# Moving the a22 weights' split parts within a partition: high part to the other weights' offset, half of the low part to its old place

## The chip, the cores and the metric

The kernel runs on one core of one Trainium2 chip. The metric is device microseconds of one execution, as the median of several executions. In the kernel, matrix products are done by TensorE (PE in the profile; PEld is its weight load), elementwise work by VectorE (DVE), ScalarE (ACT) and GpSimd (POOL). SyncE (SP), ACT and POOL issue DMA transfers. SBUF is the on-chip memory with 128 partitions; where a tile lies is a byte offset that is the same in every partition.

## The reference

One decoder block over 512 positions of 1024 channels, in float32. The part that matters here is the gated feed-forward at its end; what stands before it (norm, projection, short convolution, sparse attention, merge) is left out.

```
h  = rmsnorm(x, norm2_g)
gu = h @ w_ffn_in                       # 1024 -> 2 * 2816
g  = causal_dwconv(gu[..., :D_FF], ffn_conv_w) + ffn_conv_b
x  = x + (silu(g) * gu[..., D_FF:]) @ w_ffn_out
```

## The kernel before

Each float32 operand is split into a high part, rounded to the type that TensorE takes at full rate, and a low part, which is the rest. A product of two such operands is three matmuls: high by high, high by low and low by high. The function `dense` (lines 437, 438 and 440) issues them: first, for each tile of 128 contracted channels, weights' high part by the moving high part (L437) and by the moving low part (L438), then, for all tiles again, weights' low part by the moving high part (L440).

The first product of the feed-forward is done two feed-forward tiles (of 128 channels) at a time in a scheme of Strassen's kind: the weights of a pair are four quarters a11, a12, a21 and a22, of which four sums are formed as well, and the tokens' activations lie in seven forms in `xf_h` and `xf_l`, each four tiles of 256 columns. A pair is then seven products instead of eight; each product is 4 x 3 = 12 matmuls of 256 columns, so a pair is 84 matmuls. There are 11 steps of f (0, 2, ... 20) with two pairs each: n = 0 for the gate half and n = 1 for the up half, 22 pairs.

`ff_forms(f, n)` makes a pair's weights. Raw weights come by DMA into `wr_s`. The quarter a22 gets its own tiles: high part `th`, low part `tl`, each 512 float32 wide (2,048 bytes per partition) with two buffers, made by `dma_split` (L173, L174 and L175: an ACT copy, an ACT copy with the sign turned, and a DMA that adds the raw weights to it). a11 and a12 lie in `wh_s` and `wl_s`; the four sums lie in `sh` and `sl`. `ff_pair` then issues the seven products, and a22 comes first: eight matmuls with `th` (four tiles, each by `xf_h` and by `xf_l`) and four with `tl` (by `xf_h` alone), then a11, a12 and the sums. The pair f = 0, n = 0 is done in another order, with matmuls put between those of the product before (L1039 and L1045).

From f = 4 on, a part of the down product, `pdn`, with weights in `wh_d` and `wl_d` and 512 moving columns, stands between two pairs: 24 matmuls. The order of instructions on each engine is found by the framework's scheduler when the program is made. It leaves some early pairs interleaved with each other and with the down product; from 443.9 us on the pairs follow each other in the plain order.

The pool `pw` holds `th`, `tl`, `sh`, `sl` and some smaller tiles. Its tiles are placed in the order in which their tags are first named, one behind the other. `th` is named first, at line 903, then a gap of 48 float32 (192 bytes), so that within the pool `th` lies at byte 0 and 2,048, the gap at 4,096, `tl` at 4,288 and 6,336 and `sh` from 8,384 on. The other weights are at the same offset modulo 512 as `tl` and `sh`.

```
pw = ctx.enter_context(tc.tile_pool(name="pw", bufs=1, side="left"))
pw.tile([P, D // 2], F32R, name="th_", tag="th", bufs=2)
const([P, 48], "gap_w", F32, pw)
```

Of the kernel before, what the change touches and what calls it, by code (L numbers as in the profile page):

```python
# [11 lines left out]
F32 = mybir.dt.float32  # L12
F32R = mybir.dt.float32r
# [5 lines left out]
P = 128  # L19
D = 1024  # L20
# [65 lines left out]
def tile_block(ctx: ExitStack, tc: tile.TileContext, xT, pos, par, par2, w_tok, w_a3, w_gate, w_ao, w_bo, w_o,  # L86
# [13 lines left out]
    def const(shape, name, dt=F32, pool=sb):  # L100
        return pool.tile(shape, dt, name=name, tag=name)
# [64 lines left out]
    def split(h, l, v):  # L166
        hi = nc.scalar.activation(h, v, AF.Copy)  # L167
        nc.vector.tensor_sub(l, v, h.bitcast(F32))  # L168
        return hi

    def dma_split(h, l, raw, src, dst=None):

        nc.scalar.activation(h, raw, AF.Copy)  # L173
        nc.scalar.activation(l, raw, AF.Copy, scale=-1.0)  # L174
        nc.gpsimd.dma_start(l if dst is None else dst, src, accum_op=ALU.add)  # L175

    def ring(name):
        return (wf.tile([P, D], F32R, name=f"wh_{name}", tag="wh", bufs=NWF),
                wf.tile([P, D], F32R, name=f"wl_{name}", tag="wl", bufs=NWF))

    def raw_tile(name):
        return wf.tile([P, D], F32, name=f"wr_{name}", tag="wr", bufs=NRAW)
# [717 lines left out]
    xf_h = const([P, 4, 7, TH], "xf_h", F32R, px)  # L900
    xf_l = const([P, 4, 7, TH], "xf_l", F32R, px)
    pw = ctx.enter_context(tc.tile_pool(name="pw", bufs=1, side="left"))
    pw.tile([P, D // 2], F32R, name="th_", tag="th", bufs=2)
    const([P, 48], "gap_w", F32, pw)

    def x_forms(k, v):
        nc.vector.tensor_sub(v[:, T1:T3 + 1], v[:, 1:4:2], v[:, 0:2])
# [57 lines left out]
        nc.scalar.activation(cv, cv, AF.Silu)  # L965

    HALF_D = D // 2

    def ff_forms(f, n):

        nm = f"{n}_{f}"
        raws = {}
        for m in (1, 0):
            raws[m] = raw_tile(f"s{nm}{m}")
            nc.sync.dma_start(raws[m], w_ff[f + m, n])
        a11, a12 = raws[0][:, 0:HALF_D], raws[0][:, HALF_D:]
        a21, a22 = raws[1][:, 0:HALF_D], raws[1][:, HALF_D:]
        form = {}
        h = pw.tile([P, HALF_D], F32R, name=f"th{nm}", tag="th", bufs=2)
        l = pw.tile([P, HALF_D], F32R, name=f"tl{nm}", tag="tl", bufs=2)  # L980
        dma_split(h, l, a22, w_ff[f + 1, n][:, HALF_D:])
        form["a22"] = (h, l)
        h, l = ring(f"s{nm}")
        dma_split(h, l, raws[0], w_ff[f, n])
        form["a11"] = (h[:, 0:HALF_D], l[:, 0:HALF_D])
        form["a12"] = (h[:, HALF_D:], l[:, HALF_D:])

        def put(i, j, v):
            h = pw.tile([P, D], F32R, name=f"sh{i}{j}{nm}", tag="sh", bufs=NSQ)
            l = pw.tile([P, D], F32R, name=f"sl{i}{j}{nm}", tag="sl", bufs=NSQ)  # L990
            split(h, l, v)
            form[i] = (h[:, 0:HALF_D], l[:, 0:HALF_D])
            form[j] = (h[:, HALF_D:], l[:, HALF_D:])

        s = {}

        def pair(i, j):
            v = pw.tile([P, D], F32, name=f"s{i}{j}{nm}", tag="sf", bufs=NSF)
            s[i], s[j] = v[:, 0:HALF_D], v[:, HALF_D:]
            return v  # L1000

        v = pair(2, 3)
        nc.vector.tensor_sub(s[3], a11, a21)
        nc.vector.tensor_sub(s[2], a22, s[3])
        put(2, 3, v)
        v = pair(4, 1)
        nc.vector.tensor_sub(s[4], a12, s[2])
        nc.vector.tensor_add(s[1], a21, a22)
        put(4, 1, v)
        return form  # L1010
# [51 lines left out]
    def ff_strassen(f, between):  # L1062
        u = u_bufs[f // 2 % NU]

        with tc.high_priority(offset=AHEAD if f == 0 else 0):
            form = ff_forms(f, 0)
        ff_pair(f, 0, u[:, :, 2:], form, late=f == 0 or None)
        between()
        nc.vector.tensor_tensor(u[:, :, 2:], u[:, :, 2:], r2two, op=ALU.mult)
        cv = pair_tile(f"cv{f}", "cv")  # L1070
        for m in range(2):
            conv_silu(f + m, cv[:, m], u[:, m])
        nc.vector.tensor_tensor(cv, cv, r2two, op=ALU.mult)
        up = pair_tile(f"up{f}", "up")
        ff_pair(f, 1, up, ff_forms(f, 1))

        between()
        nc.vector.tensor_tensor(up, up, cv, op=ALU.mult)
        for m in range(2):
            h, l = a_tiles(f + m)  # L1080
            split(h, l, up[:, m])
# [108 lines left out]
```

## Time and profile before

| what | value |
|---|---|
| median of 3 executions | 697.33 us (697.29 to 697.89) |
| profiled execution, its own time | 696.92 us |
| its span, first to last instruction | 695.1 us |
| VectorE busy | 511.7 us (74%) |
| ScalarE busy | 436.7 us (63%) |
| GpSimd busy | 248.7 us (36%) |
| HBM read and written | 111.55 MB and 12.58 MB, 179 GB/s over the span |

The page gives, for each engine, the time in which it was busy. Matmuls overlap: one lasts longer than the time between two starts, so a matmul's duration is not its cost in a dense stream. The timeline gives the starts in microseconds from the span's begin; the difference of two starts, divided by the number of matmuls between them, is what one costs. Rows of the timeline merge consecutive matmuls of one line (x4 is four). The sums over stretches give busy time and count of each engine in a window. The words after the operation name the tile written and the tiles read, output first, with buffer numbers left out.

### The profile page before, as it was taken

The page shows a single profiled execution, that of the slowest core. Times are in us where ns is not written, and L with a number is a line of the kernel's source. Part 1 is how long each engine was busy: PE and PEld are TensorE (multiplying, and loading weights), DVE is VectorE, ACT ScalarE, POOL GpSimd, SP SyncE. Part 2 cuts the span into 40 slices and gives each one's busy share as a digit, 9 for nine tenths or more (in the row PEclk, how much of TensorE's full clock was granted, in tenths as well). Part 3 has the DMA queues.
Part 4 walks back from the last instruction along what each step waited for, and adds up shares of the span by engine and source line. Part 5 has one row for each costly group of instructions (what it writes and reads, how often), then busy time and mean ns, then how long its engine had stood idle before and what let it go on. Part 6 is the DMA issues. An engine that isn't in the chain of part 4 may idle for free.

```text
span 695.1 us, 11268 instructions
## 1 busy us (share of the span) xinstructions
PE 689.2 (99%) x4111; PEld 614.5 (88%) x4111; DVE 511.7 (74%) x897; ACT 436.7 (63%) x776; POOL 248.7 (36%) x247
## 2 busy tenths in 40 slices
PE   9999999999999999999999999999999999999997
PEld 9999888887878888788889999999999999999986
DVE  6987886766566546475888999898787787877543
ACT  7635654878888866535776857665566655566530
POOL 4041443477788867462112212121122211112110
PEclk9999999999999999999999999999999999999999
DMA  8333686568666654563586977997877979775665
GB/s 268 113 98 122 170 194 145 132 240 237 222 222 228 195 169 124 193 229 118 130 198 160 219 192 167 245 218 180 215 173 180 210 172 227 174 175 112 132 137 152
DMA packets 57623, 124.87 MB, mean 180 GB/s; under 512 B 5344, under 2 KB 21088, under 8 KB 57568
## 3 DMA queue, kind: packets, MB, share of 16 engines
q1 hardware_dynamic: 35648, 79.39, 35.3%
q0 software_dynamic: 14848, 32.51, 27.4%
q10 hardware_dynamic: 7072, 12.26, 5.5%
q8 instruction: 32, 0.52, 0.3%
q14 instruction: 23, 0.19, 0.1%
HBM read 111.55 MB, written 12.58 MB: 179 GB/s over the span
## 4 chain that ended last, share of the span: by engine, by line
PE 95%; ACT 2%; DMA 1%; POOL 1%; DVE 1%; issue 0%; SPq 0%; ACTq 0%; POOLq 0%
PE p L438 10%; PE p L437 10%; PE p L440 10%; PE pdn L438 6%; PE pdn L437 6%; PE pdn L440 6%; PE pg L437 4%; PE pg L438 4%; PE pg L440 3%; PE pa L438 3%; PE pa L437 3%; PE pa L440 3%; PE po L438 2%; PE po L440 2%; PE po L437 2%; PE pj_s L269 2%
## 5 line engine op out<-in xcount | busy, mean ns | idle before, releaser
L437 PE MATMUL p<-xf_h,sh 128*128 128x256 f32 x336 | 80.6, 277 | 0.0
L438 PE MATMUL p<-xf_l,sh 128*128 128x256 f32 x336 | 80.5, 276 | 0.0
L175 POOL DMA_DIRECT2D wl_s<-in_w_ff_dram x22 | 19.6, 891 | 156.1 <-ACT wl_s L174 154.8
L438 PE MATMUL pdn<-al,wh_d 128*128 128x512 f32 (+1 forms) x176 | 68.5, 389 | 0.0
L437 PE MATMUL pdn<-ah,wh_d 128*128 128x512 f32 (+1 forms) x176 | 68.3, 389 | 0.0
L438 PEld LDWEIGHTS p<-xf_l,sh 128*128 128x128 f32 x336 | 63.1, 188 | 0.0
L437 PEld LDWEIGHTS p<-xf_h,sh 128*128 128x128 f32 x336 | 63.1, 188 | 0.0
L167 ACT ACTIVATE sh<-s 128x1024 fp32r<-128x1024 f32 x44 | 46.3, 1055 | 25.3 <-PE p L438 22.4
L168 DVE TENSOR_TENSOR sl<-s,sh 128x1024 fp32r<-128x1024 f32 x44 | 53.5, 1218 | 8.7 <-ACT sh L167 8.6
L173 ACT ACTIVATE wh_s<-wr_s 128x1024 fp32r<-128x1024 f32 x22 | 23.3, 1060 | 56.9 <-PE pdn L438 54.3
L750 POOL TENSOR_TENSOR tn_e<-tn_e,ph 128x512 fp32r<-128x512 f32 x40 | 51.2, 1294 | 16.2 <-ACT ph L749 16.0
L440 PE MATMUL p<-xf_h,sl 128*128 128x256 f32 x336 | 52.2, 277 | 0.0
L175 POOL DMA_DIRECT2D wl_d<-in_w_dn_dram x22 | 26.7, 1212 | 71.3 <-ACT wl_d L174 71.3
L437 PE MATMUL pg<-xg_h,wh_g 128*128 128x512 f32 x128 | 50.1, 392 | 0.0
L438 PE MATMUL pg<-xg_l,wh_g 128*128 128x512 f32 x128 | 50.1, 391 | 0.0
L440 PE MATMUL pdn<-ah,wl_d 128*128 128x512 f32 (+1 forms) x176 | 47.5, 388 | 0.0
L440 PEld LDWEIGHTS p<-xf_h,sl 128*128 128x128 f32 x336 | 44.7, 188 | 0.2
L1109 DVE TENSOR_TENSOR x<-x,pdn 128x512 f32<-128x512 f32 x47 | 32.0, 682 | 15.9 <-PE pdn L440 15.3
L150 POOL TENSOR_TENSOR wl_g<-wr_g,wh_g 128x1024 fp32r<-128x1024 f32 x16 | 38.5, 2405 | 10.4 <-ACT wh_g L148 9.7
L438 PE MATMUL p<-xf_l,wh_s 128*128 128x256 f32 x168 | 40.6, 277 | 0.0
L437 PE MATMUL p<-xf_h,wh_s 128*128 128x256 f32 x168 | 40.5, 277 | 0.0
L175 POOL DMA_DIRECT2D tl<-in_w_ff_dram x22 | 19.7, 894 | 57.3 <-ACT tl L174 49.7
(367 smaller groups left out, 2117.5 us busy)
## 6 DMA issues: line engine op xcount, KB each, us to landing
wr_s<-in_w_ff_dram SPq DMA_DIRECT2D x44, 512.0 KB, 5.0
wl_s<-in_w_ff_dram POOLq DMA_DIRECT2D x22, 512.0 KB, 7.8
wr_d<-in_w_dn_dram ACTq DMA_DIRECT2D x22, 512.0 KB, 8.3
wl_d<-in_w_dn_dram POOLq DMA_DIRECT2D x22, 512.0 KB, 9.0
wr_g<-in_w_gate_dram SPq DMA_DIRECT2D x16, 512.0 KB, 4.0
wr_a<-in_w_a_dram SPq DMA_DIRECT2D x12, 512.0 KB, 3.7
tl<-in_w_ff_dram POOLq DMA_DIRECT2D x22, 256.0 KB, 7.6
td_e<-e SPq DMA_DIRECT2D x16, 256.0 KB, 4.4
```

The lines of the kernel that those rows point to most:

```text
L150: e.tensor_sub(lo[:, 0:n], raw[:, 0:n], hi[:, 0:n].bitcast(F32))
L167: hi = nc.scalar.activation(h, v, AF.Copy)
L168: nc.vector.tensor_sub(l, v, h.bitcast(F32))
L173: nc.scalar.activation(h, raw, AF.Copy)
L175: nc.gpsimd.dma_start(l if dst is None else dst, src, accum_op=ALU.add)
L269: nc.tensor.matmul(acc, xg_h[:, k, ts_], wh, start=k == 0, stop=False)
L437: ops.append(nc.tensor.matmul(acc, wh, xh, start=first and i == 0, stop=False))
L438: ops.append(nc.tensor.matmul(acc, wh, xl, start=False, stop=False))
L440: nc.tensor.matmul(acc, wl, xh, start=False, stop=last and i == len(units) - 1)
L750: nc.gpsimd.tensor_sub(pl, pt, ph.bitcast(F32))
L1109: nc.vector.tensor_add(xj, xj, acc)
```

## The change

The order in which tags are named at the head of `pw` changes: first a tile of the new tag `tl0`, then the gap, then the two buffers of `th`. The low part gets two tags with one buffer each, `tl0` and `tl1`, used in turn by the calls of `ff_forms`, in place of one tag with two buffers. Within the pool `tl0` then lies at byte 0, the gap at 2,048, `th` at 2,240 and 4,288, and `tl1` at 6,336, where the second buffer of `tl` lay. `sh` and all behind it stay where they are. Since the calls alternate between n = 0 and n = 1, `tl0` holds the low part of every pair with n = 0 and `tl1` that of every pair with n = 1. The instructions and their order stay the same.

```
     pw = ctx.enter_context(tc.tile_pool(name="pw", bufs=1, side="left"))
+    pw.tile([P, D // 2], F32R, name="tl_", tag="tl0", bufs=1)
+    const([P, 48], "gap_w", F32, pw)
     pw.tile([P, D // 2], F32R, name="th_", tag="th", bufs=2)
-    const([P, 48], "gap_w", F32, pw)
...
     HALF_D = D // 2
+    sides = []
...
         h = pw.tile([P, HALF_D], F32R, name=f"th{nm}", tag="th", bufs=2)
-        l = pw.tile([P, HALF_D], F32R, name=f"tl{nm}", tag="tl", bufs=2)
+        l = pw.tile([P, HALF_D], F32R, name=f"tl{nm}", tag=f"tl{len(sides) % 2}", bufs=1)
+        sides.append(nm)
```

## The prediction

> **What bounds the kernel now.** I read the page first, then the groups by line and form, then TensorE's timeline with sums over stretches. The page:
>
> ```profile
> span 695.1 us, 11268 instructions
> PE 689.2 (99%) x4111; PEld 614.5 (88%) x4111; DVE 511.7 (74%) x897; ACT 436.7 (63%) x776; POOL 248.7 (36%) x247
> PEclk9999999999999999999999999999999999999999
> PE 95%; ACT 2%; DMA 1%; POOL 1%; DVE 1%; issue 0%; SPq 0%; ACTq 0%; POOLq 0%
> ```
>
> TensorE is busy 99% of the span at full granted clock, and 95% of the chain that ends last is matmuls. So what counts is how far apart consecutive matmuls start. Nothing else in this change can move the end: no instruction is added, removed or reordered. By form:
>
> ```profile
> L437 PE MATMUL p<-xf_h,sh 128*128 128x256 f32 x336 | 80.6, 277 | 0.0
> L437 PE MATMUL p<-xf_h,th 128*128 128x256 f32 x84 | 21.0, 281 | 0.0
> L438 PE MATMUL p<-xf_l,th 128*128 128x256 f32 x84 | 21.1, 282 | 0.0
> L440 PE MATMUL p<-xf_h,tl 128*128 128x256 f32 x84 | 13.1, 277 | 0.0
> ```
>
> The same matmul on the same moving data lasts 277 ns with weights in sh or tl, 281 to 282 ns with th, and none of these rows has idle time before it. What sets th apart is its place. In the program's allocation the pool pw starts at byte 94,496 of a partition, so both th buffers start at 288 modulo 512; the gap of 192 bytes behind them puts tl, sh and sl at 480 modulo 512, where wh_s and wl_s also lie. The moving rows of xf_h and xf_l all start at 288. Durations overlap, so I use the starts. A steady pair of feed-forward tiles:
>
> ```profile
> 443.90 0.28 PE L437 MATMUL p<-xf_h,th 128*128 128x256 f32 x1
> ...
> 444.85 0.62 PE L440 MATMUL p<-xf_h,tl 128*128 128x256 f32 x4
> 445.30 0.28 PE L437 MATMUL p<-xf_h,wh_s 128*128 128x256 f32 x1
> ...
> 453.46 0.39 PE L437 MATMUL pdn<-ah,wh_d 128*128 128x512 f32 x1
> ```
>
> The sums over its two stretches (us, length, then busy time and count for each engine; a PE count can include a matmul still running at the start, so I count loads, PEld, where they differ):
>
> ```profile
> 443.89:444.84 0.95, 0.94 (x8) 0.94 (x8) 0.00 (x0) 0.00 (x0) 1.00 1.12 276
> 444.84:453.45 8.61, 8.61 (x78) 8.59 (x76) 1.29 (x2) 0.36 (x1) 1.00 0.88 198
> ```
>
> Eight th matmuls take 0.95 us, 119 ns each; the 76 behind them take 8.61 us, 113.3 ns each. The first impression is therefore that th's offset costs 5.5 ns a matmul and that moving it is a gain. **The trace has a second fact that speaks against that**: the same 480 weights also run at 118 ns in places.
>
> ```profile
> 406.11 0.39 PE L438 MATMUL pdn<-al,wh_d 128*128 128x512 f32 x1
> 406.34 0.40 PE L437 MATMUL p<-xf_h,wh_s 128*128 128x256 f32 x2
> ...
> 411.76 0.28 PE L437 MATMUL p<-xf_h,th 128*128 128x256 f32 x1
> ...
> 412.71 0.62 PE L440 MATMUL p<-xf_h,tl 128*128 128x256 f32 x4
> ```
>
> ```profile
> 406.33:411.75 5.42, 5.41 (x46) 5.41 (x46) 1.01 (x2) 0.39 (x1) 1.00 0.95 231
> 411.75:412.70 0.95, 0.95 (x10) 0.95 (x9) 0.51 (x1) 0.00 (x0) 1.00 1.05 379
> 412.70:417.68 4.98, 4.98 (x46) 4.96 (x44) 1.18 (x3) 0.00 (x0) 1.00 0.34 105
> 424.08:428.44 4.36, 4.35 (x37) 4.31 (x36) 1.07 (x2) 0.23 (x1) 1.00 0.39 161
> 431.18:432.48 1.30, 1.29 (x11) 1.25 (x10) 0.48 (x1) 0.00 (x0) 1.00 1.00 170
> 435.23:438.41 3.18, 3.17 (x27) 3.13 (x26) 0.00 (x0) 0.00 (x0) 1.00 1.07 286
> ```
>
> At 406.34 a pair continues straight behind a down product (pdn, 512 columns) with weights at 480, not with th. All 46 matmuls up to th take 5.42 us, 117.8 ns each. Then come eight th, and behind them the 44 matmuls with weights at 480 take 4.98 us, 113.2 ns each. Three further stretches, at 424.09, 431.19 and 435.24, also begin behind a pdn with weights at 480 and have no th: 37, 11 and 27 matmuls at 117.8, 118 and 117.8 ns (4.36/37, 1.30/11, 3.18/27), without one return to 113. The entry at 424.09 is made by tl itself:
>
> ```profile
> 423.63 0.62 PE L440 MATMUL pdn<-ah,wl_d 128*128 128x512 f32 x2
> 424.09 0.52 PE L440 MATMUL p<-xf_h,tl 128*128 128x256 f32 x3
> 424.44 0.28 PE L437 MATMUL p<-xf_h,wh_s 128*128 128x256 f32 x1
> ```
>
> Three tl matmuls take 0.35 us, 117 ns each: the same tile that follows th at 113. So 256-column matmuls with weights at 480 have two rates, a short one (113.3 ns) and a long one (117.8 ns); a 512-column matmul ahead of them leaves them in the long one, it keeps itself up, and a full run of th at 288 ends it. Th's offset costs 8 x 5.5 = 44 ns a pair, and buys the short rate for the 76 matmuls behind. That th does this is my reading; the trace does not show what inside TensorE it is.
>
> **The change part by part.** (1) th moves from 288 to 480. (2) tl of n = 0 (tl0, as ff_forms is called alternately for n = 0 and n = 1) moves from 480 to 288. (3) tl of n = 1 (tl1) keeps the old second tl buffer's place. sh, sl and all behind them stay, since the pool's head keeps its 8,384 bytes. ACT and POOL write the same tiles as long before use as now; they are hidden behind the 99% busy TensorE, and of a change of their time I count nothing.
>
> *Steady pairs, n = 1.* The second and the last steady pair start, behind a pdn, at
>
> ```profile
> 458.93 0.28 PE L437 MATMUL p<-xf_h,th 128*128 128x256 f32 x1
> ...
> 654.27 0.28 PE L437 MATMUL p<-xf_h,th 128*128 128x256 f32 x1
> ```
>
> The period is 458.93 - 443.90 = 15.03 us, and (654.27 - 443.90)/15.03 = 14, so there are 15 such pairs, each opened by th; the first and the last are n = 1, hence 8 of n = 1 and 7 of n = 0. With everything at 480, a pair of n = 1 is just what stands at 406.34 and 424.09: it enters long and nothing ends it. 84 x 0.1178 = 9.90 us against 453.46 - 443.90 = 9.56: **+0.34 us, times 8 = +2.7 us**. Bounds for one pair: -0.04 us (th simply becomes 8 x 113.3) and +0.34.
>
> *Steady pairs, n = 0.* th runs long (8 x 117.8 = 0.94 us, as now), then four tl0 matmuls at 288 stand where tl was. Does half a run of the odd offset still end the long rate? The rows speak both ways:
>
> ```profile
> 361.20 0.28 PE L438 MATMUL p<-xf_l,th 128*128 128x256 f32 x1
> 361.32 0.28 PE L437 MATMUL p<-xf_h,wh_s 128*128 128x256 f32 x1
> ...
> 361.79 0.28 PE L1039 MATMUL p<-xf_h,sh 128*128 128x256 f32 x1
> ```
>
> That is the end of a run of four th matmuls (two weight tiles, each used twice), and the four wh_s behind it still take 0.47 us, 118 ns each. Against it, the stretch from 411.75 shows that a full run entered from the long rate ends it, and tl0 loads four different tiles as a full run does. I take it that it does, narrowly: four tl0 at 119 instead of 113.3 are +0.02 us, th 0.01 less: **7 x 0.01, about +0.1 us**. If it does not, the 72 others add 72 x 4.5 = 0.32 us, so 0.34 x 7 = +2.4 us.
>
> *Pairs ahead of the steady ones.* th1 at 411.76 no longer ends the long stretch: 8 + 44 = 52 matmuls at 117.8 are 6.13 us instead of 0.95 + 4.98 = 5.93: **+0.2 us**. Three pairs with no pdn ahead (f = 2 both, f = 4 n = 0) are at the short rate already, and there th only costs:
>
> ```profile
> 374.07:404.49 30.42, 30.42 (x268) 30.39 (x267) 5.99 (x10) 1.49 (x4) 1.00 0.91 219
> 398.10 0.28 PE L437 MATMUL p<-xf_h,th 128*128 128x256 f32 x1
> ...
> 399.06 0.62 PE L440 MATMUL p<-xf_h,tl 128*128 128x256 f32 x4
> ```
>
> (268 matmuls in 30.42 us, 113.5 ns on average with the th among them.) Eight th take 0.96 us; at the short rate they take 0.91: 3 x -0.05; two of the three are n = 0 and get tl0 at 288, 2 x +0.03. **-0.1 us.** At 424.09 the three tl become 288 and may shorten the 34 behind them by 4.5 ns: 0 to -0.15, I take **-0.1**.
>
> *The down products.* Entered from the long rate they cost what they cost now:
>
> ```profile
> 438.42 0.40 PE L437 MATMUL pdn<-ah,wh_d 128*128 128x512 f32 x1
> ...
> 440.27 1.07 PE L440 MATMUL pdn<-ah,wl_d 128*128 128x512 f32 x4
> ```
>
> ```profile
> 455.30 0.39 PE L440 MATMUL pdn<-ah,wl_d 128*128 128x512 f32 x1
> ```
>
> Eight take 1.85 us behind the long rate and 455.30 - 453.46 = 1.84 behind the short one: **0**, at most 8 x 0.01 = +0.1.
>
> Sum: 2.7 + 0.1 + 0.2 - 0.1 - 0.1 = **+2.8 us**. The profiled execution took 696.92 us (its span of 695.1 and 1.8 around it), 0.41 below the median of 697.33; I add to the median: **700.1 us**.
>
> The Trainium skill, "TensorE: Matmul & The Clock Gate", section "Step-by-step: what each phase is for", says that TensorE reads moving data and weights through two independent ports, so that loading the next weights takes nothing from the running matmul. By that rule an address could not matter and the time would stay; the 119 ns of th beside 113.3 of tl disagree with it.
>
> **The rivals.** *tl0 does not end the long rate* (the row at 361.32 speaks for it): 2.7 + 2.4 + 0.2 - 0.1 = +5.2, 702.5 us. *Only th's own cost counts*, the case that is not slower: behind a pdn th at 480 drops to the short rate by itself. It decides at the first matmuls of each steady pair. For it: no th at 480 has been seen there, and all four stretches that I lean on lie between 406 and 438 us. Against: all four entered long, with wh_s, sl and tl alike. Price: 15 x -0.04 and 3 x -0.05, with tl0 at +0.02 to 0.03 in about 10 pairs: -0.6 + 0.25 - 0.2 is about -0.6, so 696.7 us. *Placement does nothing*, the differences coming from the order of the products: 697.3 us; against it the long and short tl. That the change doesn't do what it says is part of this one. Or something between: some pairs of n = 1 fall back, +1 to +2, or the long rate reaches further, +6.
>
> **How the numbers follow.** Forecast (tl0 ends it) 0.42, own range 699.5 to 700.9; tl0 does not 0.33; only th's cost 0.13; nothing 0.04; between or beyond 0.08. The range from 698.6 to 703.2 holds the first two and most of the last, about 0.8. A measurement tells about 0.2%, 1.4 us, from no change: slower holds 0.79 (first two and half of the last), same 0.19 (th's cost, nothing, a little), faster 0.02.
>
> **What would show it.** th's first eight starts in a steady pair of n = 1: 0.94 us and the 76 behind at 117.8, pair length 9.90; if they fall to 113 within the eight, the second rival holds. In n = 0: the 72 behind tl0 at 113.3 (forecast) or 117.8. The span from 374 to 404 should shrink by 0.1. The forecast is wrong if th at 480 enters short, or if the stages before 347 us, which I count as unchanged, move.

## The result, and the profile after

The changed kernel takes 703.07 us (median of 6 runs, 702.17 to 703.58) beside 697.31 us of the kernel before on the same chip (6 runs, 695.81 to 698.02): ratio 1.0082, 95% interval 1.0069 to 1.0095. It is slower by 5.8 us. The profiled execution took 702.17 us. Its page, first the span and the busy time, the clock of TensorE and the chain that ended last:

```profile
span 700.3 us, 11268 instructions
PE 694.9 (99%) x4111; PEld 620.6 (89%) x4111; DVE 512.7 (73%) x897; ACT 436.8 (62%) x776; POOL 248.9 (36%) x247
PEclk9999999999999999999999999999999999999999
PE 89%; DMA 3%; ACT 3%; POOL 2%; DVE 1%; issue 1%; SPq 0%; ACTq 0%; POOLq 0%; DVEq 0%
```

The other engines' busy times are as before, the clock is full, and TensorE still fills 99% of the span, with the same 4111 matmuls. It is 5.7 us longer busy: the matmuls themselves start further apart. The groups by form show which:

```profile
L437 PE MATMUL p<-xf_h,sh 128*128 128x256 f32 x336 | 82.8, 279 | 0.0
L437 PE MATMUL p<-xf_h,th 128*128 128x256 f32 x84 | 20.9, 280 | 0.0
L438 PE MATMUL p<-xf_l,th 128*128 128x256 f32 x84 | 20.9, 280 | 0.0
L440 PE MATMUL p<-xf_h,tl 128*128 128x256 f32 x84 | 13.5, 281 | 0.0
```

The matmuls with th, which was moved to 480, last 1 or 2 ns less than their 281 to 282. Those with sh, which kept its offset modulo 512, last 2 ns longer, over 336 matmuls a line. So most of what grew is not what was moved, but what stands behind it. TensorE's timeline in the second steady pair (n = 0; start, duration, line, operation, count):

```profile
459.31 0.28 PE L437 MATMUL p<-xf_h,th 128*128 128x256 f32 x1
...
460.25 0.65 PE L440 MATMUL p<-xf_h,tl 128*128 128x256 f32 x4
460.74 0.28 PE L437 MATMUL p<-xf_h,wh_s 128*128 128x256 f32 x1
...
469.22 0.39 PE L437 MATMUL pdn<-ah,wh_d 128*128 128x512 f32 x1
```

and the sums over stretches of the same execution, for the tile p alone (stretch, its length, then TensorE's matmuls and its weight loads, as busy time and count; a count can include one still running from before):

```profile
372.78:404.34 31.56, 31.55 (x268) 31.51 (x267) 5.57 (x10) 1.13 (x3) 1.00 0.86 210
406.18:411.60 5.42, 5.41 (x46) 5.41 (x46) 1.01 (x2) 0.39 (x1) 1.00 0.95 206
411.60:412.55 0.95, 0.95 (x10) 0.95 (x9) 0.32 (x1) 0.00 (x0) 1.00 1.11 310
412.55:417.72 5.17, 5.17 (x46) 5.14 (x44) 1.37 (x3) 0.00 (x0) 1.00 0.58 178
443.93:444.87 0.94, 0.93 (x8) 0.93 (x8) 0.00 (x0) 0.00 (x0) 1.00 1.11 253
444.87:453.82 8.95, 8.95 (x78) 8.92 (x76) 1.37 (x2) 0.36 (x1) 1.00 1.00 225
459.30:460.24 0.94, 0.93 (x8) 0.93 (x8) 0.00 (x0) 0.00 (x0) 1.00 0.37 105
460.24:460.73 0.49, 0.49 (x6) 0.49 (x5) 0.00 (x0) 0.00 (x0) 1.00 0.85 309
460.73:469.21 8.48, 8.48 (x74) 8.44 (x72) 1.38 (x2) 0.38 (x1) 1.00 0.95 216
```

In a pair of n = 1 the 76 matmuls behind th now take 8.95 us, 117.8 ns each, where they took 8.61, 113.3 each. In a pair of n = 0, four tl0 at 288 take 0.49 us, and the 72 behind them 8.48 us, again 117.8 ns each. No steady pair returns to the short rate, of either n. The last steady pair starts at

```profile
659.16 0.28 PE L437 MATMUL p<-xf_h,th 128*128 128x256 f32 x1
```

so 14 periods take 659.16 - 443.94 = 215.22 us, where they took 654.27 - 443.90 = 210.37: +4.85, or 15.37 - 15.03 = 0.34 a period.

The other large piece is the long stretch without a down product. In both kernels it is entered behind the second of two 512-column matmuls that have nothing to do with the change. Before:

```profile
373.74 0.40 PE L419 MATMUL pr_n<-dg_n,ones 128*128 128x512 f32 x1
373.97 0.28 PE L438 MATMUL p<-xf_l,wh_s 128*128 128x256 f32 x1
...
404.50 0.39 PE L437 MATMUL pdn<-ah,wh_d 128*128 128x512 f32 x1
```

and after, from 372.79 to 404.35 (the first of the rows above). The same 268 matmuls took 30.53 us before and take 31.56 now: 113.9 and 117.8 ns each.

| stretch | before | after | difference |
|---|---|---|---|
| up to the first of the 268 | 373.97 | 372.79 | -1.18 |
| the 268 | 30.53 | 31.56 | +1.03 |
| first down product | 1.84 | 1.84 | 0 |
| 98 matmuls from 406 us on | 11.35 | 11.54 | +0.19 |
| on to the first steady pair | 26.21 | 26.21 | 0 |
| 14 steady periods | 210.37 | 215.22 | +4.85 |
| last pair and end of the span | 40.83 | 41.14 | +0.31 |

The sum is 5.20 us, the difference of the two spans (700.3 - 695.1). The first line has other work in it, which the change doesn't touch; the kernel before alone varied by 2.2 us over its six runs, and I put this line down to that: TensorE's first matmul with th already starts at 359.67 after and 360.84 before, so the difference was there before TensorE read a moved tile. Without it the changed stages cost 6.4 us in these two executions. The 1.03 of the long stretch is known from this one execution of each kernel; whether the others entered it at the same rate is not on record.

A correction to what stands ahead, the prediction included: tl1 does not lie where the second tl buffer lay. Its tag is named later than those of sf (the pool's tile for the float32 sums), sh, sl and p1 (a small result tile), so in the allocation of the changed program it lies behind these, at byte 134,624 of a partition, and they lie 2,048 bytes lower than before. All of them are still at 480 modulo 512. The first experiment, in which sh, sl and tl lie where they lay, has the same time within 0.1 us, so this plays no part that shows.

### The profile page after: what moved, and what is told of

It is laid out like the page before. It is cut to its first block, busy times and chain, and to the rows that moved or that the text cites. A ratio compares the mean times of both kernels' runs of the same rounds, so it can differ in the third digit from the quotient of the medians.

```text
span 700.3 us, 11268 instructions
## 1 busy us (share of the span) xinstructions
PE 694.9 (99%) x4111; PEld 620.6 (89%) x4111; DVE 512.7 (73%) x897; ACT 436.8 (62%) x776; POOL 248.9 (36%) x247
## 4 chain that ended last, share of the span: by engine, by line
PE 89%; DMA 3%; ACT 3%; POOL 2%; DVE 1%; issue 1%; SPq 0%; ACTq 0%; POOLq 0%; DVEq 0%
PE p L440 10%; PE p L437 10%; PE p L438 10%; PE pdn L437 6%; PE pdn L438 6%; PE pdn L440 6%; PE pg L438 3%; PE pg L437 3%; PE pg L440 3%; PE pa L438 3%; PE pa L437 3%; PE pa L440 3%; PE po L438 2%; PE po L437 2%; PE po L440 2%; PE pj_s L269 2%
## 5 line engine op out<-in xcount | busy, mean ns | idle before, releaser
L437 PE MATMUL p<-xf_h,sh 128*128 128x256 f32 x336 | 82.8, 279 | 0.0
L438 PE MATMUL p<-xf_l,sh 128*128 128x256 f32 x336 | 82.8, 279 | 0.0
```

Source lines behind the costliest of these rows:

```text
L437: ops.append(nc.tensor.matmul(acc, wh, xh, start=first and i == 0, stop=False))
L438: ops.append(nc.tensor.matmul(acc, wh, xl, start=False, stop=False))
```

## The experiments

The theory in all of them: a run of matmuls with weights at the moving rows' own offset (288, distance 0) ends the long rate for what follows; the change took that run away (th to 480) and put one in its place (tl0) that doesn't do it. The rival at first: tl0's new place, not th's, is what costs. The sums over stretches below are for the tile p, columns as above. "Behind" means the rest of the pair.

**th moved, tl not.** The gap goes ahead of th; th and both tl lie at 480, nothing at 288.

```
+    const([P, 48], "gap_w", F32, pw)
     pw.tile([P, D // 2], F32R, name="th_", tag="th", bufs=2)
-    const([P, 48], "gap_w", F32, pw)
```

> th and all of tl at 480 like every other weight (the gap lies first in the pool); nothing at 288. Theory A (a run of eight th at 288 ends the long rate; tl0 at 288 is neither harm nor help): all 15 steady pairs long, 9.90 us each, time within 0.5 us of the changed kernel's 703.07. Theory B (tl0 at 288 is what makes the pairs long, or the changed places of sh and tl1): the pairs fall to 113 ns, about 9.52 us each, time about 696.7.

703.05 us (4 runs) beside 697.10 (13 runs): ratio 1.0081, interval 1.0056 to 1.0105, the same as the change itself. The long stretch and a steady pair of n = 0:

```profile
373.49:405.06 31.57, 31.55 (x268) 31.52 (x267) 6.12 (x10) 1.49 (x4) 1.00 0.88 214
460.01:469.91 9.90, 9.89 (x84) 9.85 (x83) 1.38 (x2) 0.39 (x1) 1.00 0.91 215
```

9.90/84 = 117.9 ns from the first matmul to the last. So tl0's place neither costs nor saves anything that the time shows; moving th costs it all, and th at 480 behind a pdn does not enter the short rate by itself.

**Both tl at 288, th at 480.**

```
+    pw.tile([P, D // 2], F32R, name="tl_", tag="tl", bufs=2)
+    const([P, 48], "gap_w", F32, pw)
     pw.tile([P, D // 2], F32R, name="th_", tag="th", bufs=2)
-    const([P, 48], "gap_w", F32, pw)
```

> th at 480, tl at 288 in every pair (n = 0 and n = 1). Theory A: four tl in a row do not end the long rate in any pair; steady pairs 9.90 to 9.92 us, span about 700.5 to 701.5. Theory C (a run of four ends it when it comes in every pair, as the state is carried over the down product): pairs 9.57 us, span about 695.

703.20 us (one run). The 72 matmuls behind the four tl, and the long stretch:

```profile
461.76:470.24 8.48, 8.48 (x74) 8.45 (x72) 1.38 (x2) 0.39 (x1) 1.00 0.90 201
374.99:405.45 30.46, 30.45 (x268) 30.41 (x267) 5.58 (x10) 1.49 (x4) 1.00 0.90 219
```

Four tl at 288 in every pair leave them all long (8.48/72 = 117.8). But the long stretch ran short here (113.7) with th at 480: it was short from its entry on, so the entry can give either rate.

**th and tl at 288**, twelve matmuls in a row.

```
     pw.tile([P, D // 2], F32R, name="th_", tag="th", bufs=2)
+    pw.tile([P, D // 2], F32R, name="tl_", tag="tl", bufs=2)
     const([P, 48], "gap_w", F32, pw)
```

> th and tl both at 288: twelve matmuls in a row at the odd offset, then wh_s at 480. Theory A1 (the length of the run decides, eight or more end the long rate): 12 x 119 + 72 x 113.3 ns = 9.59 us a steady pair, 0.03 above before's, time 697.3 + 0.5 = 697.8. Theory A2 (what decides is the step from th to tl, where the next product starts on the other moving row; the step from tl to wh_s does not end it): all pairs long, 12 x 119 + 72 x 117.8 = 9.91 us, time about 703.

697.47 us (10 runs), ratio 0.9999, interval 0.9988 to 1.0011: the time of before. What stands behind three runs of twelve, one in a steady pair and two in the long stretch:

```profile
461.89:470.05 8.16, 8.16 (x74) 8.14 (x72) 1.20 (x2) 0.39 (x1) 1.00 0.96 220
381.41:389.54 8.13, 8.13 (x71) 8.13 (x70) 1.71 (x3) 0.36 (x1) 1.00 0.64 174
390.97:399.13 8.16, 8.16 (x74) 8.16 (x73) 1.45 (x3) 0.39 (x1) 1.00 1.07 233
```

72 matmuls in 8.16 us are 113.3 ns: the release does not need tl to follow th. The second row I had not expected: 69 matmuls in 8.13 us, 117.8 ns, behind twelve at 288 that were entered from the long rate. So a full run does not always end it, although here it is one place of the long stretch; all 15 steady pairs are released.

**th at 288 for n = 0 only**, by one tag for each n.

```
-    pw.tile([P, D // 2], F32R, name="th_", tag="th", bufs=2)
+    pw.tile([P, D // 2], F32R, name="th_", tag="th0", bufs=1)
     const([P, 48], "gap_w", F32, pw)
+    pw.tile([P, D // 2], F32R, name="th__", tag="th1", bufs=1)
...
-        h = pw.tile([P, HALF_D], F32R, name=f"th{nm}", tag="th", bufs=2)
+        h = pw.tile([P, HALF_D], F32R, name=f"th{nm}", tag=f"th{n}", bufs=1)
```

> th at 288 in the pairs of n = 0 and at 480 in those of n = 1, tl at 480. Theory A: each pair for itself, 7 steady pairs of n = 0 at 9.56 us and 8 of n = 1 at 9.90; span 695.1 + 2.7 + 0.2 = 698, and up to 1.2 more if the stretch from 374 to 404 us goes long too. Rival (a pair left at the short rate leaves the next one short, across the down product): all pairs at 9.52 to 9.56, span 695.

700.55 us (one run). A pair of n = 1, whole, and what stands behind th in the next, of n = 0:

```profile
444.75:454.64 9.89, 9.88 (x84) 9.85 (x83) 1.37 (x2) 0.36 (x1) 1.00 0.99 234
461.07:469.68 8.61, 8.61 (x78) 8.59 (x76) 1.20 (x2) 0.39 (x1) 1.00 0.96 208
```

117.7 and 113.3 ns, in turn: each pair is decided by its own th, and nothing is carried over a down product.

**Fewer of th at 288**: directly behind pdn, a run of four for n = 0 and of six for n = 1; the rest of th at 480.

```
+    pw.tile([P, 560], F32R, name="th0_", tag="th0", bufs=1)
+    pw.tile([P, 592], F32R, name="th1_", tag="th1", bufs=1)
...
+            at = lambda k: k * P if wf_ != "a22" else (k * P + 48 * (k > 1) if n == 0 else 208 + k * P if k < 3 else 0)
```

> How long must the run at 288 be? In the pairs of n = 0 only th's first two tiles lie at 288 (a run of four matmuls, each tile used twice, as at 361 us), in those of n = 1 its first three (a run of six); the rest of th and all else at 480. th's copy is two ACT instructions instead of one. If it is the number of matmuls and eight are needed: both kinds long, 9.90 us a steady pair, span about 701. If a run of six is enough and four is not: n = 1 about 9.57, n = 0 9.90, span about 698. If four matmuls of th are enough (so that tl0 failed as its tiles are used once each): all pairs about 9.55, span about 695.

706.80 us, which can't be compared: the high part is copied by two ACT instructions here, the order of the early products changed with it, and TensorE stands idle for 2.5 us between 415 and 435 us. In the steady pairs, the 76 matmuls behind th, n = 0 and n = 1:

```profile
465.01:473.97 8.96, 8.96 (x78) 8.92 (x76) 1.38 (x2) 0.39 (x1) 1.00 0.89 219
480.38:489.34 8.96, 8.96 (x78) 8.92 (x76) 1.38 (x2) 0.36 (x1) 1.00 0.71 143
```

Both long (117.9): directly behind pdn neither four nor six end it. In the same run, though, a run of six in the long stretch does end it, the th of f = 2, n = 1 at 388.61, although it is entered from the long rate. The matmuls ahead of it and those behind it:

```profile
380.01:388.60 8.59, 8.59 (x75) 8.59 (x74) 2.18 (x4) 0.37 (x1) 1.00 0.70 196
389.32:398.16 8.84, 8.84 (x80) 8.84 (x79) 1.69 (x3) 0.39 (x1) 1.00 1.05 225
```

By the starts, 73 matmuls fill the first row, 117.7 ns each, and 78 the second, 113.3 ns. So six can be enough.

**tl0 twice**: in the changed kernel, tl0's four matmuls of n = 0 are issued twice, so that eight at 288 stand behind th. The low part of a22 counts twice in n = 0.

```
+        for r_ in range(1 + again):
+            for i, (wh, wl, xh, xl) in enumerate(units):
+                nc.tensor.matmul(acc, wl, xh, start=False, stop=last and i == len(units) - 1 and r_ == again)
```

> The changed kernel, but in the pairs of n = 0 (from f = 2 on) the four matmuls with tl0 are issued twice, so that a run of eight stands at 288; the product of a22's low part counts twice in these pairs. The changed kernel's four are followed by 72 matmuls at 117.8 ns. If the length of the run decides: the 72 behind the eight at 113.3 ns, a pair of n = 0 takes 8 x 117.8 + 8 x 119 + 72 x 113.3 = 10.05 us with its 88 matmuls. If it needs th's way of using a tile twice, or tl as the next tile: 117.8 behind them, 10.37 us. Pairs of n = 1 stay at 9.90 in both.

707.92 us (one run). Behind the eight in a steady pair of n = 0:

```profile
462.66:471.15 8.49, 8.49 (x74) 8.45 (x72) 1.38 (x2) 0.39 (x1) 1.00 0.89 183
```

Still long: 117.9, and so in all seven steady pairs of n = 0. But in the same run two other eights of tl0 that are entered from the long rate end it, at 379.56 and at 424.40. Behind the first:

```profile
380.51:388.32 7.81, 7.81 (x71) 7.81 (x70) 1.70 (x3) 0.36 (x1) 1.00 0.59 151
```

That is 69 matmuls, 113.2 ns each. So the length alone does not decide, nor does the rate that stands ahead.

**tl0 ahead of th, once and twice.** What was left open is whether tl0 fails by its length, by where it is entered from, or because each of its tiles is used once and th's twice. In the changed kernel the four matmuls of tl0 (n = 0) are put ahead of th, directly behind pdn, and issued once or twice (twice counts the low part twice).

```
+        for r_ in range(ahead):
+            for i, (wh, wl, xh, xl) in enumerate(units):
+                nc.tensor.matmul(acc, wl, xh, start=first and i == 0 and r_ == 0, stop=False)
         for i, (wh, wl, xh, xl) in enumerate(units):
...
-        for i, (wh, wl, xh, xl) in enumerate(units):
-            nc.tensor.matmul(acc, wl, xh, start=False, stop=last and i == len(units) - 1)
```

> The changed kernel, with the four low-part matmuls of the a22 product of every n = 0 pair (weights tl0 at 288) issued ahead of the eight of th instead of behind them. Read: the matmuls behind the four in the steady n = 0 pairs. Theory L (a run of four is too short, wherever it stands): long, 118 ns, pair 9.9 us, as before the move, total 703. Theory E (tl0 fails only because it is entered from the long rate, one matmul run behind the down product): standing directly behind pdn it ends the long rate, 113.3 ns behind, pairs of n = 0 about 9.56 us, total about 700.7. The 4-run of the earlier run with th cut short stayed long, so L is expected here for the pair; pairs of n = 1 are long by both.

> As the run with tl0's four ahead, but these four issued twice: a run of eight single-use tiles at 288 directly behind pdn; the a22 low part is counted twice in n = 0. Theory 'eight at 288 directly behind pdn end the long rate': 113.3 ns behind the eight, pair of n = 0 of 88 matmuls about 8 x 0.119 + 80 x 0.1133 = 10.0 us. Theory 'only th's pattern does it, each tile used twice in a row (xf_h, then xf_l)': 118 ns behind, pair 10.4 us. The eight of single-use tiles standing behind th in an earlier run did not end it, so release here would put that down to the entry from the long rate.

703.06 us and 704.60 us (one run each). Once: behind the four in a steady pair, and in the long stretch behind the four at 398.74:

```profile
460.78:470.19 9.41, 9.41 (x82) 9.38 (x80) 1.38 (x2) 0.39 (x1) 1.00 0.85 209
399.21:405.33 6.12, 6.12 (x54) 6.08 (x52) 1.12 (x2) 0.36 (x1) 1.00 0.61 208
```

Twice: behind the eight in a steady pair, and behind the eight at 378.80 and 398.73:

```profile
461.99:471.05 9.06, 9.06 (x82) 9.04 (x80) 1.38 (x2) 0.39 (x1) 1.00 0.83 168
379.75:388.83 9.08, 9.08 (x79) 9.08 (x78) 2.43 (x5) 0.36 (x1) 1.00 0.66 177
399.67:405.56 5.89, 5.89 (x54) 5.87 (x52) 1.36 (x2) 0.36 (x1) 1.00 0.60 202
```

80 matmuls in 9.41 us are 117.6 ns, in 9.06 us 113.3. Eight single-use matmuls directly behind pdn end the long rate; four in the same place don't. At 398.7 us the two kernels stand in the same place too, entered nearly alike, and again four leave it long (6.12/52 = 117.7) and eight end it (5.89/52 = 113.3). At 378.80 eight don't (77 matmuls in 9.08 us, 117.9). So single use is not the reason; **length and entry both count**. What the entry is shows in the distances of consecutive starts, in ns, taken from the start times of the trace:

```
                             ahead  | the run at 288                   | behind
before            443.90     226    | 116 117 120 121 117 117 120 121  | 113 113 114
tl0 twice ahead   461.05     226    | 116 118 119 121 117 117 120 121  | 114 113 113
tl0 twice ahead   398.73     115    | 117 118 120 120 117 118 120 120  | 114 113 113
tl0 twice ahead   378.80     118    | 121 120 124 117 118 121 120 120  | 122 118 115
tl0 twice behind  461.71     118    | 121 120 124 117 118 121 120 120  | 122 118 115
tl0 once ahead    460.31     226    | 116 118 119 120                  | 113 118 118
tl0 once ahead    398.74     116    | 119 119 121 116                  | 118 117 119
after             460.25     118    | 121 120 124 117                  | 118 118 118
tl0 twice behind  424.40     117    | 118 119 121 117 117 120 120 121  | 113 114 113
th, n = 0 only    398.75     117    | 118 120 120 117 118 120 120 120  | 114 113 113
six of th         388.61     117    | 118 119 121 117 117 121          | 113 114 113
```

Eights with the same start go the same way, matmul by matmul, whichever tile they load. Entered behind a pdn, or behind a spacing of 115 ns, eight end it. Entered as after's tl0 is, at 118 with 121 as its first spacing, neither four nor eight do. The last three rows show that the spacing ahead alone does not tell: all three are entered at 117 and end it. What divides the runs is their own first spacing. The traces with weights at 480 and 288 have eighteen runs of eight or twelve entered from the long rate: seven begin with 116 to 118 ns and end it, eleven begin with 119 to 121 and don't. Directly behind a pdn the first spacing is 115 to 117, and all of them end it. This was read off the traces afterwards; no run set the first spacing, and what sets it is not shown. The length counts beside it: behind a pdn runs of four and six begin with 115 or 116 too and end nothing.

**Other distances.** To see what other places of the moving rows do, the rows of xf were shifted and all the pairs' weights put at 480 by the two gaps (80 and 48 elements before; for distance 256, 64 and 64):

```
-    const([P, 80], "gap_x", F32, px)
+    const([P, 64], "gap_x", F32, px)
...
+    const([P, 64], "gap_w", F32, pw)
     pw.tile([P, D // 2], F32R, name="th_", tag="th", bufs=2)
-    const([P, 48], "gap_w", F32, pw)
```

> All weights at 480 as in the run before with nothing at 288, but xf_h and xf_l moved 64 bytes down, from 288 to 224: weights and moving rows are 256 apart instead of 192. Theory P (the distance of weights and moving rows modulo 512 decides whether a long rate exists): another rate than 117.8 ns in the steady pairs, 113 to 120. Theory Q (only a step in the weights' offset matters, not the distance): 117.8 ns, 9.90 us a pair, time about 703.

> As the run with distance 256, with xf moved 64 bytes up, to 352: distance 128. Theory P: another rate than 117.8 ns in the steady pairs, between 113 and 120, not the same as at 256. Theory Q: 117.8 ns, about 703.

> As the run with distance 256, with xf moved 128 bytes down, to 160: distance 320. Theory P: another rate than 117.8 ns in the steady pairs; if the two streams only ever meet at small distances it is 113.3 throughout, 9.52 us a pair and a time near 696. Theory Q: 117.8 ns, about 703.

> All weights at 480, xf at 256: distance 224, between 192 (two rates, 113.3 and 117.8) and 256 (120 throughout). If the short rate ends at 192 (a wide forbidden zone around 256): 120 ns, time about 706.5. If 224 is like 192: long rate, 117.8, about 703. If it is past both meeting points: 113.3 throughout, about 696.

> All weights at 480, xf at 320: distance 160, between 192 (two rates) and 128 (119 to 120). Like 128: about 119.9 ns, time about 706.5. Like 192: 117.8, about 703. Short throughout: 113.3, about 696.

> The kernel before with all weights of the pairs at 480 and the moving rows xf shifted to 416, distance 64. Distances 128, 160 and 256 ran at about 120 ns, 224 at 116.7, 192 and 320 at 113.3 or 117.8. Theory 'a distance's own spacing, near 120 as at 0 and 128': total about 706 to 707, pair 10.1 us. Rival 'the interference falls away between 0 and 128': spacing of 113.3 or below throughout, pair 9.5 us, total 696 or less, which would be a kernel faster than both.

> As the run at distance 64, with the moving rows at 384, distance 96. Same two theories: 119 to 120 ns throughout and 706 to 707, or 113.3 or below and 696 or less; two rates as at 192 would give 117.8 in the steady pairs and about 703.

> As the run at distance 64, with the moving rows at 448, distance 32. Same theories: 119 to 120 ns and 706 to 707, or a short spacing and 696 or less.

One run each. The steady pair is from the first th to the next pdn on the timeline, 84 matmuls; the last column is the 268 matmuls of the long stretch, where they ran at another rate than the steady pair.

| weights less moving rows, mod 512 | time, us | a steady pair, us | ns each | long stretch |
|---|---|---|---|---|
| 32 | 704.05 | 460.75 to 470.69, 9.94 | 118.3 | |
| 64 | 700.43 | 458.15 to 468.04, 9.89 | 117.7 | 372.98 to 403.37, 113.4 |
| 96 | 704.20 | 460.72 to 470.69, 9.97 | 118.7 | |
| 128 | 706.51 | 461.01 to 471.09, 10.08 | 120.0 | 373.64 to 405.43, 118.6 |
| 160 | 707.59 | 462.04 to 472.12, 10.08 | 120.0 | |
| 192 (th and tl at 480, above) | 703.05 | 460.02 to 469.92, 9.90 | 117.9 | |
| 224 | 701.47 | 460.12 to 469.92, 9.80 | 116.7 | |
| 256 | 706.85 | 461.68 to 471.76, 10.08 | 120.0 | |
| 320 | 701.09 | 458.81 to 468.70, 9.89 | 117.7 | 372.79 to 403.17, 113.4 |

The same matmuls on the same data take 116.7 to 120.0 ns in a steady pair by the place of the moving rows alone, and four of the distances, 64, 128, 192 and 320, were seen with two rates: at 128 it is 120.0 behind a pdn and 118.6 in the long stretch, at the other three 117.7 to 117.9 behind a pdn and 113.3 to 113.4 in other stretches. The weights lay at 480 in every row, so that nothing but the difference counts is not shown. The hope that a distance between 0 and 128 has the short rate throughout fell. None beats the kernel before.

**The release at another distance.** xf and th at 160, the rest at 480: th at distance 0 as in before, the others at 320.

```
-    const([P, 80], "gap_x", F32, px)
+    const([P, 48], "gap_x", F32, px)
     pw.tile([P, D // 2], F32R, name="th_", tag="th", bufs=2)
-    const([P, 48], "gap_w", F32, pw)
+    const([P, 80], "gap_w", F32, pw)
```

> As before, but xf and th lie 128 bytes lower, at 160: th has distance 0 to the moving rows as in the kernel before, all other weights 320 instead of 192. At 320 the two rates were seen too, and the down product behind a pair at the long rate started without its slow head. If a run of th ends the long rate here too: steady pairs 9.56 us, time between 696 and 697.5, at best 0.4 less than before if the heads go. If it does not: 9.90 us, about 702.

702.18 us (4 runs) beside 697.28 (7 runs), ratio 1.0080, interval 1.0059 to 1.0100. Behind th in a steady pair:

```profile
460.84:469.79 8.95, 8.95 (x78) 8.92 (x76) 1.38 (x2) 0.39 (x1) 1.00 0.97 228
```

117.8: eight th at distance 0 don't end the long rate of distance 320. The release in the kernel before does not carry over to other distances: it is shown for 0 and 192 alone.

## Why the prediction was right or wrong

The sign was right, the size half: +2.8 us was forecast, +5.76 came. 702.5 us, the price of the first rival ("tl0 does not end the long rate"), is 0.6 below the measured time; it lacks the long stretch, which cost +1.03 in the profiled execution, so part of that agreement may be luck.

**Steady pairs, n = 1, +2.7: right.** 9.89 us a pair as forecast (9.90), +0.33 each.

**Steady pairs, n = 0, +0.1: wrong, and this is the step that failed.** "I take it that it does, narrowly" rested on two arguments: tl0 loads four different tiles, as a full run does, and the full run at 411.75 ended a long stretch although it was entered from the long rate. The first is refuted: four different tiles directly behind pdn don't end it, eight do. The second overlooked that the entry counts: the run at 411.75 began with a spacing of 118 ns, after's tl0 in the steady pairs begins with 120 or 121, from where not even eight end it. The row at 361.32, four th and no release, was the better witness, and I quoted it and decided against it. The term should have been 7 x 0.34 = +2.4; the pair at 459.31 measures 9.91 against 9.56, +0.35.

**The stretch from 406 to 417 us, +0.2: right** (+0.19).

**The three pairs of the long stretch, -0.1: wrong.** I counted them as short already and th as a cost alone. The stretch can be entered at either rate: 113.7 ns on average with th at 480 and tl at 288, 117.8 with all of them at 480 and in the changed kernel. Which one comes can be read ahead of it: in the ten traces with weights at 480 or 288 and the rows at 288, the last 512-column matmul ahead is followed after 232 or 233 ns where the stretch is short at its entry (two traces) and after 226 or 227 where it is long (eight). What sets this is not shown. In after it was entered long, nothing ended it, and it cost +1.03. (The 113.5 ns that the prediction gives for this stretch divides 30.42 us by 268, but the window holds 267 starts; it is 113.9.) In this execution it used up nearly all of the 1.18 us by which the earlier stages happened to be shorter.

**The entry at 424.09, -0.1, and the down products, 0:** from 417.69 to 443.90 before and 417.73 to 443.94 after are 26.21 us each; three tl0 saved nothing, so that the -0.1 did not come, and the down products cost what they cost before.

**The rivals.** "Only th's own cost counts" fell with the first experiment: with nothing at 288 every steady pair stays long. "Placement does nothing" fell with the same run. The rule of two independent ports, which I weighed from the Trainium skill ("TensorE: Matmul & The Clock Gate", "Step-by-step: what each phase is for"), would, as I read it, have every row of the table of distances equal; they differ by up to 3.3 ns a matmul (9.80 to 10.08 us a pair), so the place of the operands does set the spacing here.

Shown, then: th at distance 0 directly behind pdn brings the short rate back in the kernel before, moving it adds 0.34 us to each steady pair, and tl0 can't replace it: four are too few even directly behind pdn, and where tl0 stands not even eight do it. Not shown is what inside TensorE, or between it and the memory, keeps up the two rates, what sets the first spacing of a run, and why six sufficed once but not behind pdn.

## What to carry to other kernels

In a dense stream of matmuls with a weight load each, look at the distances of starts by stretch before you move a tile: a tile that looks slow may be what keeps its neighbours fast. Where a long rate ends only under a condition, price the case in which the condition fails as seriously as the other, and take the nearest row (here four matmuls, no release) before an argument by likeness. A single execution's luck at an entry can hide a microsecond, so compare stretch by stretch.

## What the runs showed of the hardware

- The spacing of 256-column matmuls with a weight load each depends on where weights and moving rows lie within a partition. With the weights at 480 modulo 512 it was, in the steady pairs and at full granted clock, 116.7 ns at a distance of 224, 120.0 at 128, 160 and 256, and 113.3 or 117.8 at 192.
- At 64, 128, 192 and 320 two rates exist for the same stream. Each keeps itself up: at 192, 268 matmuls took 31.57 us with nothing at another offset among them, at 64 the same 268 took 30.39 us.
- At 192, eight matmuls at distance 0 directly behind a 512-column matmul switch the long rate to the short one; four and six there do not. Entered from the long rate, eight and twelve did so in the seven places where their first spacing was 116 to 118 ns, and not in the eleven where it was 119 to 121 (69 matmuls in 8.13 us behind twelve); six did it once (78 matmuls in 8.84 us behind them).
- The Trainium skill, "TensorE: Matmul & The Clock Gate", section "Back-to-back issue gap", gives the gap of an isolated matmul by its columns alone, 262 cycles for 256 columns, which at its 2.4 GHz is 109.2 ns. The stream here is not that case, since every matmul has its own weight load, and no run reached the figure: 113.3 ns is the shortest steady spacing, and the columns alone did not set it.
